# A two-block transformer kernel on one core: the first projection cut at 336, another order of the mixer's stages, one planner round

## The chip, the cores and the metric

One NeuronCore of a Trainium2 chip runs the whole program. The metric is the time of one execution on the device in microseconds (us). Each version is run several times and the median is taken; one more execution is taken with the hardware profiler, and all rows below come from it.

## The reference, cut to what matters

256 tokens of width 1024 go through a first block and then through a second block that is two layers deep. The change touches the first block's mixer and the end of the program:

```
h = rmsnorm(x, norm_mix_g)
c_q, c_kv, k_r, u_ssm, x_q, gate_logits = split(h @ w_in)    # 384, 256, 32, 512, 512, 3 x 1024 columns
y_a = mla_branch(c_q, c_kv, k_r, ...) @ w_o_mla              # 8 heads, causal
y_b = s5_branch(u_ssm, ...) @ w_o_ssm                        # state space scan, GELU, gated unit
y_c = cross_branch(x_q, mem, ...) @ w_o_cross                # 4 heads over 256 memory rows
gates = sigmoid(gate_logits + b_gate)
x = x + (gates[0] * y_a + gates[1] * y_b + gates[2] * y_c) @ w_out
x = x + convolved_swiglu(rmsnorm(x))
for l in range(2):
    x = x + 0.5 * swiglu(...); x = x + mixer2(...); x = x + 0.5 * swiglu(...)
return rmsnorm(x, g_final)
```

All is float32. The first 672 columns of `w_in` are c_q, c_kv and k_r.

## The kernel before, in words

The tokens are two tiles of 128 rows. Every product is made in three matmuls: a weight and an activation are each split into a high part (rounded to the matmul's format, a copy on ScalarE, ACT) and a low part (the rest, a subtraction on VectorE, DVE), and high x high, high x low and low x high are added up in PSUM. Weights come from memory in pieces of 512 KB (`weights`, five buffers `raw`, all issued by SyncE, SP) and are split into tiles `wh` and `wl`, of which 34 are in use at most; all working tiles share 65 slots.

The program isn't issued as it is written. The functions of `Ctx` only record operations (`Program.add`), with their engine, an assumed cost and what they depend on. At the end `issue` has a planner (`plan`) find an order: `backward` gives each operation a due time, `forward` places operations engine by engine in a simulated time, the most urgent first, as far as buffers allow. With two rounds this is done twice, the second time from the order of the first. The result is one fixed order for each engine's queue. So the string `ORDER`, which lists the stages of the first mixer in the order in which they are recorded, moves instructions on all engines.

The stages in `ORDER` (function `mixer1`, L1305): `h0` and `h1` are four heads each of the attention with latents (a product with `w_q_b` from the latent cq, a product with `w_kv_b` from ckv, head norms, rotary terms, scores `ms`, softmax `p`, output `mo`). `k0` and `k1` are the keys and values of the memory rows, `x0` the cross attention (`cs`, `co`). `s0` and `s1` are the halves of the state space branch: its maps `xB`, `x0`, `cT` are made on DVE and GpSimd (POOL) from small tables and transposed on TensorE (PE); u is moved by 16 small DMAs into `u4`; the products `se` give the state inputs, DVE turns them (`sp`), scans them (`sv`) and turns them back (`sg`), and PE multiplies `sg` with `cT` into `yb`. `g0`, `g1`, `g2` are the gates: 192 matmuls of 256 columns each (`proj_T`, tile `pt`), which depend on h and their weights alone. `b0`, `b2` are the first two branches into the merge.

Ahead of the stages `mixer1` loads x, warms PE up with matmuls of zeros (`warm_up`, L623), makes h (`first_norm`), and computes the first 672 columns with `proj`, the 512 columns of u with `proj_T`, the latents (`mla_latents`), the query of the cross attention and the norm of the memory rows (`norm_T`). The two calls for the 672 columns:

```python
        ps = self.proj(w_in, 0, 512, rows=True)
        ps = self.proj(w_in, 512, 160)
```

At the end of the program (L1590 on) `norm_rows` scales the rows of each token tile by their gain and norm in two halves `xs`, and SP stores them.

Of the kernel before, what the change touches and what calls it, by code (L numbers as in the profile page):

```python
# [13 lines left out]
AF = mybir.ActivationFunctionType  # L14
ALU = mybir.AluOpType
# [13 lines left out]
SLOW = 1.0  # L29
ORDER = "s0 h0 k0 k1 x0 h1 s1 g0 g1 g2 b0 b2"  # L30
STEPS = [1, 2, 3, 4] + [4 * q for q in range(1, 9)] + [32 * p for p in range(8)]
# [43 lines left out]
class Program:  # L75
# [281 lines left out]

    def issue(self, tc, rounds=2):
        with tc.manual_schedule():
            for i in self.plan(rounds):  # L360
                self.ops[i].call()
# [44 lines left out]
class Ctx:  # L406
# [40 lines left out]
    def load(self, dst, src, kind="load"):  # L447
        n = int(np.prod(src.shape))
        self.prog.add("sp", lambda: self.nc.sync.dma_start(dst, src), n * 4 / self.prog.DMA_RATE, [src], [dst], kind)


# [124 lines left out]

    def norm_rows(self, halves, g):

# [7 lines left out]
        r = self.row_rstd(ss)  # L586
        for b in range(2):
            self.dve.tensor_scalar(out=xs[b], in0=xs[b], scalar1=r, scalar2=None, op0=ALU.mult)
        return xs
# [33 lines left out]
    def warm_up(self, n):  # L623

        z = self.w("warm", 320).bitcast(BF16)
        self.dve.memset(z, 0.0)
        ps = self.bank("warm")
        for i in range(n):
            self.prog.add("pe", lambda: self.nc.tensor.matmul(ps, lhsT=z[:, 0:128], rhs=z[:, 128:640], start=True, stop=True),  # L629
                          430.0 if i < 9 else 220.0, [z], [ps], "first")  # L630

# [673 lines left out]
    def mixer1(self):  # L1305
# [7 lines left out]
        self.prog.ops[-1].kind = "first"  # L1313
        self.warm_up(19)
        self.parameters()
# [18 lines left out]
        self.pool.tensor_copy(out=self.identb, in_=self.ident)  # L1334
        ps = self.proj(w_in, 0, 512, rows=True)
        for t in range(2):
            self.act.copy(out=cq[t], in_=ps[t][:, 0:384])
            self.act.copy(out=ckv[t][:, 0:128], in_=ps[t][:, 384:512])
        ps = self.proj(w_in, 512, 160)
        for t in range(2):  # L1340
            self.act.copy(out=ckv[t][:, 128:288], in_=ps[t])

# [227 lines left out]
def two_block_kernel(ctx, tc, a, out):  # L1570
# [20 lines left out]
    for t in range(2):  # L1591
        xs = k.norm_rows(k.x_halves(t), g)
        for b in range(2):
            k.load(out[t * 128:t * 128 + 128, b * 512:b * 512 + 512], xs[b], "store")
    k.prog.issue(tc)
# [74 lines left out]
```

## Time and profile before

| what | us |
|---|---|
| median of 3 runs (lowest to highest) | 1574.74 (1571.79 to 1578.25) |
| the profiled execution | 1573.03 |
| its span in the profile | 1571.3 |
| PE busy in it | 1553.6 |
| DVE busy | 1025.7 |
| ACT busy | 840.1 |
| POOL busy | 101.7 |

The span is the profiled execution without what lies around it (1.7 us). Matmuls are pipelined: the next one starts before the last one has left the array, and their ends are modelled, so PE counts as busy where it is not at its peak. How many instructions start in a stretch says more. Of TensorE's clock the profile gives the granted share: 1.00 is 2.4 GHz, 0.50 is 1.2 GHz. A number in brackets behind a row of the timeline is the idle time of that engine ahead of it, with what ended it.

### The profile page before, as it was taken

The page shows a single profiled execution, that of the slowest core. Times are in us where ns is not written, and L with a number is a line of the kernel's source. Part 1 is how long each engine was busy: PE and PEld are TensorE (multiplying, and loading weights), DVE is VectorE, ACT ScalarE, POOL GpSimd, SP SyncE. Part 2 cuts the span into 40 slices and gives each one's busy share as a digit, 9 for nine tenths or more (in the row PEclk, how much of TensorE's full clock was granted, in tenths as well). Part 3 has the DMA queues.
Part 4 walks back from the last instruction along what each step waited for, and adds up shares of the span by engine and source line. Part 5 has one row for each costly group of instructions (what it writes and reads, how often), then busy time and mean ns, then how long its engine had stood idle before and what let it go on. Part 6 is the DMA issues. An engine that isn't in the chain of part 4 may idle for free.

```text
span 1571.3 us, 28497 instructions
## 1 busy us (share of the span) xinstructions
PE 1553.6 (99%) x11145; PEld 1430.9 (91%) x11145; DVE 1025.7 (65%) x1820; ACT 840.1 (53%) x1759; POOL 101.7 (6%) x204
## 2 busy tenths in 40 slices
PE   9999999999999999999999999999999999999998
PEld 7889999899989999889998999899998899989997
DVE  7896897787676545756657554665457656575543
ACT  8766665765555544555446444455345554464442
POOL 5114600000000000000000000000000000000000
PEclk9999999999999999999999999999999999999999
DMA  8556164566556656555647665466664556476650
GB/s 284 174 151 178 44 211 138 191 217 212 185 175 221 208 195 210 158 158 164 212 138 235 200 208 193 148 221 203 207 209 148 167 162 198 146 233 209 203 186 28
DMA packets 214230, 287.79 MB, mean 183 GB/s; under 512 B 13904, under 2 KB 170192, under 8 KB 214096
## 3 DMA queue, kind: packets, MB, share of 16 engines
q1 hardware_dynamic: 213952, 285.71, 57.0%
q8 instruction: 88, 1.44, 0.4%
q14 instruction: 46, 0.38, 0.1%
q10 hardware_dynamic: 144, 0.26, 0.0%
HBM read 284.36 MB, written 1.05 MB: 182 GB/s over the span
## 4 chain that ended last, share of the span: by engine, by line
PE 89%; DVE 4%; ACT 2%; DMA 2%; issue 1%; POOL 0%; POOLq 0%; DVEq 0%; ACTq 0%
PE pt L497 50%; PE acc L497 21%; PE pr L497 7%; PE up L497 4%; PE tr L522 2%; ACT wh L398 1%; DVE wl L398 1%; DMA raw<-in_w_ffn_dram 1%; DVE xs L398 1%; DMA raw<-in_w_in_dram 1%; DVE x L398 1%; PE se L497 1%; PE ms L497 0%; PE warm L629 0%; PE yb L497 0%
## 5 line engine op out<-in xcount | busy, mean ns | idle before, releaser
L398 DVE TENSOR_TENSOR wl<-raw,wh 128x512 fp32r<-128x512 f32 x1045 | 657.2, 686 | 193.9 <-ACT wh L398 184.0
L497 PE MATMUL pt<-h,wh 128*128 128x256 f32 x4224 | 736.1, 277 | 0.0
L398 ACT CAST wh<-raw 128x512 fp32r<-128x512 f32 x1045 | 578.3, 618 | 147.2 <-DMA raw<-in_w_in_dram 43.3
L497 PEld LDWEIGHTS pt<-h,wh 128*128 128x128 f32 x4224 | 642.4, 188 | 2.8 <-issue 0.2
L497 PE MATMUL pt<-h,wl 128*128 128x256 f32 x2112 | 584.1, 277 | 0.0
L497 PEld LDWEIGHTS pt<-h,wl 128*128 128x128 f32 x2112 | 397.0, 188 | 0.7 <-issue 0.5
L497 PE MATMUL acc<-wh,gh 128*128 128x512 f32 x440 | 170.6, 388 | 0.0
L497 PE MATMUL acc<-wh,gl 128*128 128x512 f32 x440 | 170.6, 388 | 0.0
L497 PE MATMUL acc<-wl,gh 128*128 128x512 f32 x440 | 170.4, 387 | 0.0
L497 PE MATMUL pr<-wh,h 128*128 128x512 f32 (+2 forms) x480 | 130.8, 355 | 2.4 <-DVE h L398 2.3
L398 ACT CAST gh<-sg 128x512 fp32r<-128x512 f32 x47 | 29.2, 621 | 147.5 <-DVE sg L398 147.5
L497 PE MATMUL up<-wh,h 128*128 128x512 f32 x320 | 100.8, 390 | 0.1
L497 PEld LDWEIGHTS pr<-wh,h 128*128 128x128 f32 x480 | 84.5, 188 | 16.0 <-DVE h L398 2.5
L497 PEld LDWEIGHTS acc<-wh,gl 128*128 128x128 f32 x440 | 82.6, 188 | 17.0
L497 PEld LDWEIGHTS acc<-wl,gh 128*128 128x128 f32 x440 | 82.5, 188 | 16.0
L497 PEld LDWEIGHTS acc<-wh,gh 128*128 128x128 f32 x440 | 82.6, 188 | 15.9
L398 DVE TENSOR_TENSOR sg<-sg,pt 128x512 f32<-128x512 f32 x36 | 24.8, 688 | 110.1 <-PE pt L497 110.1
L398 ACT ACTIVATE sg<-pt 128x512 f32<-128x512 f32 x36 | 21.5, 598 | 130.4 <-PE pt L497 130.4
L497 PE MATMUL pr<-wl,h 128*128 128x512 f32 (+2 forms) x240 | 85.0, 354 | 0.0
L398 POOL TENSOR_TENSOR rs<-s,mhalf 128x1 f32<-128x1 f32 x20 | 16.4, 820 | 961.8 <-DVE s L398 961.8
L497 PEld LDWEIGHTS up<-wh,h 128*128 128x128 f32 x320 | 59.7, 188 | 12.5 <-ACT h L398 0.6
L398 ACT ACTIVATE junk<-x 128x512 f32<-128x512 f32 x36 | 22.7, 631 | 79.1 <-DVE x L398 76.2
(352 smaller groups left out, 1639.8 us busy)
## 6 DMA issues: line engine op xcount, KB each, us to landing
raw<-in_w_ffn_dram SPq DMA_DIRECT2D x264, 512.0 KB, 5.0
raw<-in_w_in_dram SPq DMA_DIRECT2D x124, 512.0 KB, 5.0
raw<-in_w_up_dram SPq DMA_DIRECT2D x44, 512.0 KB, 4.8
raw<-in_w_out_dram SPq DMA_DIRECT2D x24, 512.0 KB, 4.8
raw<-in_w_down_dram SPq DMA_DIRECT2D x22, 512.0 KB, 4.5
raw<-in_w_mem_kv_dram SPq DMA_DIRECT2D x8, 512.0 KB, 4.5
raw<-in_w_branch_ret_dram SPq DMA_DIRECT2D x8, 512.0 KB, 3.5
raw<-in_w_o_mla_dram SPq DMA_DIRECT2D x4, 512.0 KB, 3.5
```

The lines of the kernel that those rows point to most:

```text
L398: self.prog.add(self.name, lambda: getattr(self.eng, op)(**kw), self.cost(op, kw), list(aps.values()), writes, "fast" if self.name == "dve ...
L497: self.prog.add("pe", lambda: self.nc.tensor.matmul(ps, lhsT=lhsT, rhs=rhs, start=start, stop=stop), ns, [lhsT, rhs], [ps])
L522: self.prog.add("pe", lambda: self.nc.tensor.transpose(out, src, ident), 109, [src, ident], [out])
```

## The change

Four things. The first 672 columns of `w_in` are computed as two parts of 336 columns, not as 512 and 160; the high parts are copied out of PSUM accordingly. The warm-up has 17 products of zeros, not 19. At the end, the second half of the second token tile is scaled on ACT, not on DVE, and stored from ACT's queue. `ORDER` is another one, with g0 and g1 earlier and k0, k1, x0 later, and the planner makes one round in place of two.

```diff
-ORDER = "s0 h0 k0 k1 x0 h1 s1 g0 g1 g2 b0 b2"
+ORDER = "s0 g0 h0 h1 g1 s1 k0 k1 x0 g2 b0 b2"
...
-    def issue(self, tc, rounds=2):
+    def issue(self, tc, rounds=1):
...
+    def store(self, dst, src, own):
+        eng, queue = ("aq", self.nc.scalar) if own else ("sp", self.nc.sync)
+        self.prog.add(eng, lambda: queue.dma_start(dst, src), 65536 * 4 / self.prog.DMA_RATE, [src], [dst], "store")
...
-    def norm_rows(self, halves, g):
+    def norm_rows(self, halves, g, shared=False):
...
-            self.dve.tensor_scalar(out=xs[b], in0=xs[b], scalar1=r, scalar2=None, op0=ALU.mult)
+            if shared and b == 1:
+                self.act.activation(out=xs[b], in_=xs[b], func=AF.Copy, scale=r)
+            else:
+                self.dve.tensor_scalar(out=xs[b], in0=xs[b], scalar1=r, scalar2=None, op0=ALU.mult)
...
-                          430.0 if i < 9 else 220.0, [z], [ps], "first")
+                          427.0 if i < 13 else 214.0, [z], [ps], "first")
...
-        self.warm_up(19)
+        self.warm_up(17)
...
-        ps = self.proj(w_in, 0, 512, rows=True)
+        ps = self.proj(w_in, 0, 336, rows=True)
         for t in range(2):
-            self.act.copy(out=cq[t], in_=ps[t][:, 0:384])
-            self.act.copy(out=ckv[t][:, 0:128], in_=ps[t][:, 384:512])
-        ps = self.proj(w_in, 512, 160)
+            self.act.copy(out=cq[t][:, 0:336], in_=ps[t])
+        ps = self.proj(w_in, 336, 336)
         for t in range(2):
-            self.act.copy(out=ckv[t][:, 128:288], in_=ps[t])
+            self.act.copy(out=cq[t][:, 336:384], in_=ps[t][:, 0:48])
+            self.act.copy(out=ckv[t], in_=ps[t][:, 48:336])
...
-        xs = k.norm_rows(k.x_halves(t), g)
+        xs = k.norm_rows(k.x_halves(t), g, t == 1)
         for b in range(2):
-            k.load(out[t * 128:t * 128 + 128, b * 512:b * 512 + 512], xs[b], "store")
+            k.store(out[t * 128:t * 128 + 128, b * 512:b * 512 + 512], xs[b], t == 1 and b == 1)
```

What this does to the order, at three places on DVE. First the scan of s0. Before, as DVE's queue has it from the last weight splits ahead of the scan on:

```order
L398 TENSOR_TENSOR wl<-raw,wh 128x512 x2
L398 TENSOR_TENSOR sp<-se,turn 128x512 x4
L398 TENSOR_TENSOR sp<-sp 128x512 x2
L398 SCALAR_TENSOR_TENSOR sv<-decay,sp 128x512 x2
L398 TENSOR_TENSOR sg<-sv,turn 128x512 x4
L398 TENSOR_TENSOR sg<-sg 128x512 x2
L398 TENSOR_TENSOR wl<-raw,wh 128x512 x9
```

Now (`rr` belongs to the rotary tables, `kss` to the latents, `rs_m` and `q` to the heads' norms):

```order
L398 TENSOR_SCALAR rs_m<-hs 128x4
L398 TENSOR_TENSOR sp<-se,turn 128x512 x2
L398 TENSOR_REDUCE kss<-krq 128x1 x2
L398 SCALAR_TENSOR_TENSOR rr<-rk,rr 128x32
L398 TENSOR_TENSOR sp<-se,turn 128x512 x2
L398 TENSOR_TENSOR sp<-sp 128x512 x2
L398 SCALAR_TENSOR_TENSOR sv<-decay,sp 128x512 x2
L398 TENSOR_TENSOR sg<-sv,turn 128x512 x4
L398 TENSOR_TENSOR sg<-sg 128x512 x2
```

The two splits right ahead of the scan are gone, and the splits for the gates that followed it follow later. On PE, 39 gate products stand between the last `se` and the first `yb<-sg` before, and 22 now, four of them of g1.

Second, the splits of the weights of h0 (`wl` of 384 columns is from `w_q_b`, the `wl` of 512 columns that follow are from `w_kv_b`). Before:

```order
L398 TENSOR_TENSOR wl<-raw,wh 128x384 x3
L398 TENSOR_TENSOR pw<-pw,pv 128x320
L398 TENSOR_TENSOR wl<-raw,wh 128x512
L398 TENSOR_SCALAR pk<-pw 128x320
L398 TENSOR_TENSOR wl<-raw,wh 128x512
L398 TENSOR_TENSOR pv<-pw,pk 128x320
L398 TENSOR_TENSOR wl<-raw,wh 128x512
L398 TENSOR_SCALAR pk<-pw 128x320
L398 TENSOR_TENSOR wl<-raw,wh 128x512
```

Now (`h` is the low part of the memory's rows, `pm` and `cT` are the maps of s0):

```order
L398 TENSOR_TENSOR wl<-raw,wh 128x384 x3
L398 TENSOR_TENSOR h<-tr,h 128x4x128 x4
L398 TENSOR_TENSOR pm<-sbc,pwr 128x512 x3
L398 TENSOR_TENSOR cT<-pm 64x16x16 x3
L398 TENSOR_TENSOR pm<-sbc,pwr 128x512
L398 TENSOR_TENSOR cT<-pm 64x16x16 x5
L398 TENSOR_TENSOR wl<-raw,wh 128x512 x2
```

The splits of the two weights of h0 stood four operations of the state branch's tables apart; now the memory's rows and the maps for C stand between them. On PE the two products follow each other with two gate products between them.

Third, the maps `xB` of s1, beside the softmax of h0. Before:

```order
L398 RECIPROCAL ls<-ls 128x4
L398 TENSOR_TENSOR p<-p,ls 128x512
L398 TENSOR_TENSOR xB<-pm 64x16x16 x2
L398 TENSOR_TENSOR q<-q,rs_r 128x384
L398 TENSOR_SCALAR rs_m<-hs 128x4
L398 TENSOR_TENSOR wl<-raw,wh 128x512
L398 TENSOR_TENSOR xB<-pm 64x16x16 x6
```

Now:

```order
L398 TENSOR_TENSOR xB<-pm 64x16x16
L398 TENSOR_TENSOR p<-p,ls 128x512
L398 TENSOR_TENSOR xB<-pm 64x16x16
L398 RECIPROCAL ls<-ls 128x2
L398 TENSOR_TENSOR p<-p,ls 128x512
L398 TENSOR_TENSOR xB<-pm 64x16x16 x4
L398 TENSOR_TENSOR kk<-kv,rs_r 128x4x64
L398 TENSOR_TENSOR xB<-pm 64x16x16 x2
```

The weight split `wl` between the maps is gone, and the maps have moved into the softmax of h0's second token tile. On SP the 32 moves of u, which stood in six blocks between loads of weights, stand in two blocks of 16. From the first norm behind the mixer on, PE's order is as before but for the five places where a norm begins.

## Rows read from the trace of the kernel before

**Rows 1.** The page, part 1: engine, busy us (share of the span), instructions.

```profile
PE 1553.6 (99%) x11145; PEld 1430.9 (91%) x11145; DVE 1025.7 (65%) x1820; ACT 840.1 (53%) x1759; POOL 101.7 (6%) x204
```

**Rows 2.** Busy time by windows: us, PE, PEld, DVE, ACT, POOL (instructions), granted clock, DMA.

```profile
60.00:70.00 10.00, 10.00 (x47) 8.26 (x46) 9.96 (x20) 6.32 (x27) 0.00 (x0) 1.00 0.28 83
...
130.00:140.00 10.00, 10.00 (x90) 10.00 (x89) 6.51 (x12) 7.34 (x12) 4.76 (x8) 1.00 0.64 173
140.00:150.00 10.00, 9.59 (x84) 9.34 (x83) 6.30 (x13) 6.91 (x20) 5.98 (x15) 1.00 0.44 116
150.00:160.00 10.00, 8.14 (x66) 7.45 (x66) 5.31 (x13) 5.70 (x13) 4.98 (x15) 1.00 0.28 92
160.00:170.00 10.00, 8.90 (x68) 7.87 (x66) 8.30 (x21) 4.96 (x10) 5.90 (x11) 0.67 0.18 55
```

**Rows 3.** Waits of PE: who waited for whom, us, times, longest.

```profile
PE pr L497 <- DVE h L398: 2.3, 1, 2.3
PE tr L522 <- DVE ckv L398: 1.4, 1, 1.4
```

**Rows 4.** The chain in order of time: start, us, what.

```profile
60.14 10.45 PE pr L497 x46
...
110.94 27.91 PE pt L497 x242
```

**Rows 5.** Timeline of the start: start, us, engine, line, operation, out<-in.

```profile
1.25 6.83 PE L629 MATMUL warm<-warm 128*128 128x512 bf16 x19 [1.25 <-DVE warm L392]
...
6.79 1.62 DVE L398 TENSOR_SCALAR xs<-x,rs 128x512 f32<-128x512 f32 x2 [0.73 <-POOL rs L398]
...
8.72 0.88 ACT L398 ACTIVATE h<-tr,par 128x128 fp32r<-128x128 f32 x3
...
22.63 0.27 PE L497 MATMUL pr<-wl,h 128*128 128x160 f32 x1
22.65 0.46 ACT L398 CAST wh<-raw 128x320 fp32r<-128x320 f32 x1
...
27.87 0.44 PE L497 MATMUL pt<-h,wh 128*128 128x256 f32 x2
```

**Rows 6.** Timeline around the scan of s0.

```profile
99.61 1.08 PE L497 MATMUL kT<-cT,x 128*32 128x128 f32 x32
99.61 2.48 DVE L398 TENSOR_TENSOR sp<-se,turn 128x512 f32<-128x512 f32 x4
...
101.65 2.51 PE L497 MATMUL yb<-uT,kT 128*128 128x256 f32 x16
...
108.68 2.26 PE L497 MATMUL yb<-sg,cT 128*32 128x63 f32 x128 [0.86 <-DVE sg L398]
```

**Rows 7.** Timeline of the late stage: h0's softmax and the maps of s1.

```profile
146.45 0.22 PE L497 MATMUL ms<-cmask,identb 128*128 128x128 bf16 x1
...
150.93 0.63 PE L522 MATMUL tr<-par,p 128*128 128x128 f32 x4 [1.34 <-DVE p L398]
...
156.33 0.69 DVE L398 TENSOR_TENSOR wl<-raw,wh 128x512 fp32r<-128x512 f32 x1 [3.71 <-PE pt L497]
...
157.05 0.52 POOL L392 MEMSET xB<- 128x512 f32 x1 [4.46 <-PE pt L497]
```

**Rows 8.** The end: two rows of the timeline, then the stores (duration ns min/median/max).

```profile
1565.38 0.63 ACT L398 ACTIVATE junk<-x 128x512 f32<-128x512 f32 x1 [1.84 <-DVE x L398]
...
1567.02 0.88 DVE L398 TENSOR_SCALAR xs<-xs,rs 128x512 f32<-128x512 f32 x2 [0.66 <-POOL rs L398]
...
L449 SPq DMA_DIRECT2D out_dram<-xs x4: 332/343/378, 1562.2 to 1568.0; - x4
```

**Rows 9.** Timeline where the first merge ends and the next norm begins.

```profile
277.40 0.58 ACT L398 CAST h<-tr 128x512 fp32r<-128x512 f32 x1
...
277.57 0.60 PE L522 MATMUL tr<-par,xs 128*128 128x128 f32 x4
278.03 0.49 PE L497 MATMUL up<-wh,h 128*128 128x512 f32 x1
```

## Prediction

> **What bounds the kernel now.** I read the page first: TensorE (PE) is busy for 1553.6 of 1571.3 us [rows 1], so a gain has to shorten what PE executes or close a hole in it. Then the busy time by windows, since busy time hides holes between pipelined matmuls; there the number of PE instructions says more. In 130 to 140, where PE runs gate products back to back, a window of 10 us holds 90 instructions; in 140 to 170 the three windows hold 84, 66 and 68 [rows 2]. That is 52 missing of 270, at 0.11 us each 5.8 us, and in the last of the three the granted clock is 0.67: half the clock (1.2 in place of 2.4 GHz) for about two thirds of the window, some 3.4 us of these 5.8. After 270 the windows are full; so the room lies in the first mixer, up to 215, and at the program's end. VectorE (DVE) is what PE runs after in the first 110 us: it is busy for 9.96 us of 60 to 70 [rows 2]. The waits of PE name the single places: 2.3 us for the norm of the memory rows, 1.4 us for a latent [rows 3], 1.3 us for softmax weights [rows 7].
>
> **The change, part by part.**
>
> *First 672 columns.* Before, 48 matmuls of 512 columns and 48 of 160. The chain shows 46 matmuls of 512 columns in 10.45 us, 0.227 each, and 242 of 256 in 27.91, 0.115 each [rows 4]; the 48 of 160 columns take from 22.63 to 27.87, 0.109 each [rows 5], no less than those of 256. So 48 x 0.227 + 5.24 = 16.1 us. Afterwards 96 of 336 columns; the line through 256 and 512 columns gives 0.150 each, 14.4 us. That is -1.7 us of PE work. ScalarE (ACT) and DVE split the same columns in 16 pieces in place of 11, a 320-column cast costing 0.46 us [rows 5]; the chain runs partly through them before 22 us, so I take -1.6, with 0 (they set the pace) and -2.5 (an early wait of PE goes too) as ends. The Trainium skill (TensorE: Matmul & The Clock Gate, Back-to-back issue gap) has a rule that speaks against this edit: a matmul costs its columns at 2.4 GHz plus 2.5 ns. By it 160 columns are 69 ns and both forms cost the same 13.7 us; the 0.109 measured [rows 5] decides against it.
>
> *Two products of zeros less.* They end at 8.08, the scaled rows that PE needs next are half done at 7.6, and the first split of them starts at 8.72 on ACT [rows 5]. Nothing, at best -0.4.
>
> *Last scaling on ACT, last store from ACT's queue.* The two scalings end at 1567.90, one after the other; an ACT pass over 512 columns takes 0.63 us [rows 8], so it ends at 1567.65 and its store leaves 0.25 us sooner, and without waiting for the third store's issue. -0.3, between -0.5 and 0.
>
> *One round of the planner.* From 270 on PE's order is the same but for five places where a residual is followed by a norm. Where a merge ends (three of them) the transposes of the first token tile now stand behind the last product instead of around it. The copy of h takes 0.58 us and the next product starts right behind it [rows 9]; it used to lie under the other four transposes and three products, now only under four transposes (0.44). About 0.25 us of new wait at each, some of it back because the last product ends earlier: +0.5 in all, 0 to +1.
>
> *The mixer's new order, up to the first state product.* Ahead of the products of the states s0 with C (108.68 [rows 6]) PE now has no k0 and k1 (96 x 0.227 = 21.8 us), four products of h1 less (0.9), 1.7 less from the first part, and 124 more gate products (14.3): 10.1 us less. DVE has 16 splits of k0 and k1, one of h1 and seven map operations less, at 0.62 each [rows 6] 14.9, and nine gate splits more, 5.6: 9.3 us less. DVE leads here, so PE arrives earlier and waits about 0.8 us more than now. By places: the 2.3 and 1.4 us [rows 3] go, since gate products, not k0, now follow the memory's norm, and the latents' transposes stand behind 96 products. In their place PE waits for the splits of h0's second weight, which stand on DVE behind the split of the memory's rows and the maps for C (16 operations, some 8 us by their widths). PE, which I estimate 2 us behind DVE there, has 11 products in that time (1.7 us): about 4 us. And between the last state input and the state products PE has 17 gate products fewer (2.0 us): now the scan's chain takes 99.61 to 108.68 [rows 6], against 5.9 us of cover. +1.0. PE's own work up to 108.68 adds up to 92.5 us at these durations and starts at 8.1, so its waits up to there are now 8.1 us. The ends: -3, if only the start (2 us) and this chain (3.2 us) still hold PE up, and +3, if DVE also waits for h0's loads, which now stand on SP behind two blocks of 16 moves of u, at 0.34 us of issue and more each [rows 8] 5.5 us a block.
>
> *The mixer's late stage.* This is the largest term. Before, PE stood 1.34 us for the softmax weights: 4.3 us from the last score to the transpose [rows 7], covered by 25 instructions. Now 39 gate products and 15 others (6 us) lie there; so too for the copy behind it. Then a weight split on DVE waited 3.71 us and a fill of xB on GpSimd (POOL) 4.46 us, each for PE to release a buffer [rows 7], PE came to the transposes of xB too early, and the clock fell behind them [rows 2]. In the new order no split stands on DVE between the first and the last xB, and these lie between the softmax steps of h0. I take back the clock's 3.4 us and half of the other 2.4, 4.6 together, rounded down: -4.5. The ends: 0 (waits of the same size turn up for x0, which is now last) and -7.5 (nothing is lost from 140 to 210).
>
> Sum: -1.6 + 0 - 0.3 + 0.5 + 1.0 - 4.5 = -4.9 us. The profiled execution took 1573.0 us (span 1571.3); the median of the runs shown is 1.7 higher, 1574.7, so I forecast 1569.8, -0.3%. About 0.5% (7.9 us, 1566.9 to 1582.6) is what a measurement of this kernel tells from no change.
>
> **The rivals.**
>
> *The first mixer closes up.* Every term at its good end: -2.5 - 0.4 - 0.5 + 0 - 3 - 7.5 = -13.9, 1560.8 us. For it: PE has work without dependences (g0, g1, g2) between all stages. Against it: the 60 to 70 row, where DVE has nothing left to give [rows 2], and the thinner cover of the scan.
>
> *The waits only move.* The late stage loses the same: -0.4, so 1574.3. For it: the instructions of h0, h1, x0 and s1 are the same, and the lengths of their chains too; x0 has only the branch b0 beside it. Against it: the cover counted above.
>
> *PE idles early, and the clock falls there.* Slower: around h0's second weight and in front of the state products, DVE's queue holds PE for some 4 and 3 us with nothing else issued. It decides if the clock falls in one of these holes as it did behind 150 to 160, where 66 instructions ran [rows 2]. Price: -1.6 - 0.3 + 0.5 + 3 for the waits, +3.4 for one more fall of the clock at the price of 160 to 170, and nothing gained later: +5.0, 1579.7. The Trainium skill (TensorE: Matmul & The Clock Gate, What's actually happening) has the half clock as the default that only activity lifts. The trace agrees: the granted clock falls once in mid-program, behind its two thinnest windows. Against this rival: the 2.3 us hole ahead of 58.8 [rows 3] brought no fall.
>
> **How the numbers follow.** Forecast 0.48, closing up 0.20, waits that move 0.17, early holes with the clock 0.15. All cases but closing up stay mostly within 0.5%: faster by over 0.5% comes from closing up (0.19) and from the forecast's good end (0.12), 0.31; slower by over 0.5% from the early holes' bad end and a little beyond, 0.07; the same 0.62. The range goes from 1560, the closing up, to 1581, the early holes with a margin of 1 us for the worst start; the forecast's own is 1564 to 1574.
>
> **What would show it.** Right: 160 to 170 at a full clock; about 85 or more PE instructions in each 10 us window of the late stage; no wait of PE for the memory's h; a wait of some 3 us in front of the products of the states. The first 672 columns end 1.5 us earlier. Wrong: a clock under 1 in a window before 110; PE waiting for POOL's or DVE's xB as before; a hole at x0; a changed time behind 290, where I expect no more than 1 us.

## The result, and the profile after

The changed kernel takes 1582.97 us (median of 6 runs, 1581.12 to 1587.91), the kernel before 1574.43 beside it. The ratio on record, 1.0064 with an interval of 1.0047 to 1.0081, is not the quotient of these two medians (that is 1.0054, within the interval); the table below gives it for every run. So the changed kernel is **slower by 0.6%**, where I had forecast 0.3% faster and a range up to 1581. The profiled execution took 1582.9 us, its span is 1581.1.

PE has no more to do than before [rows 1]; the page of the changed kernel, part 1:

```profile
PE 1555.1 (98%) x11143; PEld 1434.9 (91%) x11143; DVE 1024.9 (65%) x1824; ACT 842.9 (53%) x1765; POOL 99.9 (6%) x204
```

So the time went into holes. Its windows, with the columns of [rows 2]:

```profile
10.00:20.00 10.00, 8.26 (x38) 7.99 (x39) 9.34 (x30) 8.99 (x30) 3.02 (x10) 0.66 0.79 245
...
60.00:70.00 10.00, 10.00 (x85) 9.75 (x84) 2.29 (x6) 4.61 (x14) 0.00 (x0) 1.00 0.34 74
70.00:80.00 10.00, 2.40 (x8) 1.69 (x9) 9.54 (x20) 8.79 (x25) 1.72 (x4) 0.67 0.52 177
80.00:90.00 10.00, 10.00 (x59) 9.47 (x58) 6.61 (x13) 7.35 (x38) 2.07 (x6) 0.82 0.65 199
...
110.00:120.00 10.00, 9.25 (x173) 8.80 (x174) 9.28 (x21) 4.30 (x21) 6.87 (x2) 0.83 0.57 164
...
160.00:170.00 10.00, 10.00 (x91) 9.95 (x89) 3.76 (x8) 7.31 (x18) 4.53 (x12) 1.00 0.46 131
170.00:180.00 10.00, 10.00 (x90) 9.34 (x88) 6.96 (x18) 7.76 (x19) 4.05 (x8) 1.00 0.02 5
```

The late stage became what I had forecast: 91 and 90 instructions a window from 160 to 180 at the full clock, where 68 [rows 2] and 88 ran before:

```profile
170.00:180.00 10.00, 10.00 (x88) 9.90 (x88) 7.51 (x17) 6.31 (x15) 7.32 (x10) 0.98 0.01 2
```

But in the changed kernel, from 70 to 80 PE issues 8 instructions, and the granted clock is 0.67 there and 0.82 in the next window. In the window ahead of it DVE, which I had called the engine that leads, is busy for 2.29 of 10 us. The waits of PE (who for whom: us, times, longest) name the place:

```profile
PE pr L501 <- DVE wl L398: 7.6, 2, 6.3
PE up L501 <- ACT h L398: 3.2, 5, 1.3
PE yb L501 <- DVE sg L398: 2.1, 1, 2.1
```

The first is h0's second weight, the second the norms behind the merges, the third the states of s0; the waits of before that stood here are gone [rows 3]. The timeline around the first, queue by queue:

```profile
39.31 10.35 SPq L449 DMA_DIRECT2D u<-uT  x16
...
52.70 13.32 SPq L449 DMA_DIRECT2D u<-uT  x16
66.11 0.53 SPq L449 DMA_DIRECT2D raw<-in_w_q_b_dram  x1
66.75 0.38 SPq L449 DMA_DIRECT2D raw<-in_w_kv_b_dram  x1
...
68.73 0.51 ACT L398 CAST wh<-raw 128x384 fp32r<-128x384 f32 x1 [5.39 <-DMA raw<-in_w_q_b_dram]
...
69.28 0.56 DVE L398 TENSOR_TENSOR wl<-raw,wh 128x384 fp32r<-128x384 f32 x1 [7.71 <-ACT wh L398]
69.76 2.48 DVE L398 TENSOR_TENSOR h<-tr,h 128x512 fp32r<-128x512 f32 x4
...
75.86 2.18 DVE L398 TENSOR_TENSOR cT<-pm 64x256 f32<-64x256 f32 x5
78.07 1.45 DVE L398 TENSOR_TENSOR wl<-raw,wh 128x512 fp32r<-128x512 f32 x2
...
71.98 0.50 PE L501 MATMUL pr<-wh,ckvh 128*128 128x512 f32 x1 [1.25 <-ACT wh L398]
78.82 0.79 PE L501 MATMUL pr<-wl,ckvh 128*128 128x512 f32 x1 [6.35 <-DVE wl L398]
...
110.75 3.68 PE L501 MATMUL yb<-sg,cT 128*32 128x63 f32 x128 [2.10 <-DVE sg L398]
```

SP issues the 16 moves of s1's u in 13.32 us. Two of h0's three loads, those in the rows above, stand behind them; ACT waits for the first of these, and DVE, idle for 7.71 us, waits for ACT. Then DVE does the memory's rows and the maps (16 operations, 69.76 to 78), and only then splits the weight for which PE waits since 72.5. Together PE waits 7.6 us at this weight (1.25 and 6.35). Two marks sum the profile up. The products of the states start at 110.75 (108.68 before [rows 6]), although by the prediction's count PE has 8.4 us less to do ahead of them (k0 and k1 less, gates more) besides the first columns. And the first norm behind the mixer begins here, 7.5 us later than before (276.4):

```profile
283.89 1.03 PE L526 MATMUL tr<-par,xs 128*128 128x128 f32 x8
285.77 0.49 PE L501 MATMUL up<-wh,h 128*128 128x512 f32 x1 [0.84 <-ACT h L398]
```

Behind that mark come 2.4 us more: 1290.2 us to the last product, where it was 1287.8.

The start lost time as well. The first gate product, behind the 672 columns, starts at 30.04, not at 27.87 [rows 5]:

```profile
10.45 0.42 PE L501 MATMUL pr<-wh,h 128*128 128x336 f32 x1 [1.98 <-ACT h L398]
...
13.33 0.65 PE L501 MATMUL pr<-wl,h 128*128 128x336 f32 x1 [1.29 <-DVE wl L398]
...
30.04 0.39 PE L501 MATMUL pt<-h,wh 128*128 128x256 f32 x2
```

### The profile page after: what moved, and what is told of

Same layout as the page of the kernel before. It is cut to its first block, busy times and chain, and to the rows that moved or that the text cites. A ratio compares the mean times of both kernels' runs of the same rounds, so it can differ in the third digit from the quotient of the medians.

```text
span 1581.1 us, 28523 instructions
## 1 busy us (share of the span) xinstructions
PE 1555.1 (98%) x11143; PEld 1434.9 (91%) x11143; DVE 1024.9 (65%) x1824; ACT 842.9 (53%) x1765; POOL 99.9 (6%) x204
## 4 chain that ended last, share of the span: by engine, by line
PE 89%; DVE 3%; DMA 2%; ACT 1%; issue 1%; POOL 0%; POOLq 0%; ACTq 0%; SPq 0%; DVEq 0%
PE pt L501 48%; PE acc L501 20%; PE pr L501 7%; PE up L501 7%; PE tr L526 2%; DVE wl L398 1%; DMA raw<-in_w_ffn_dram 1%; DMA raw<-in_w_in_dram 1%; PE yb L501 1%; DVE x L398 1%; PE ms L501 0%; PE glu L501 0%; PE ry L501 0%; ACT wh L398 0%; DVE xs L398 0%
## 5 line engine op out<-in xcount | busy, mean ns | idle before, releaser
L398 DVE TENSOR_TENSOR wl<-raw,wh 128x512 fp32r<-128x512 f32 (+2 forms) x1050 | 656.2, 682 | 207.0 <-ACT wh L398 191.0
L398 ACT CAST wh<-raw 128x512 fp32r<-128x512 f32 (+2 forms) x1050 | 578.3, 616 | 144.4 <-DMA raw<-in_w_ffn_dram 51.9
```

Source lines behind the costliest of these rows:

```text
L398: self.prog.add(self.name, lambda: getattr(self.eng, op)(**kw), self.cost(op, kw), list(aps.values()), writes, "fast" if self.name == "dve ...
```

## The experiments

Of every run the table gives the ratio to the kernel before, timed beside it on the same chip, and two marks of its profile: where the first norm behind the mixer begins, and from there to the last product. The marks are of one execution each, and executions of one kernel differ in their granted clock (last section), so a few us between two marks can be that; the ratios come from all runs.

| kernel | ratio (interval) | median us | mixer ends | behind |
|---|---|---|---|---|
| before | 1 | 1574.4 | 276.4 | 1287.8 |
| the change | 1.0064 (1.0047 to 1.0081) | 1583.0 | 283.9 | 1290.2 |
| late_moves | 1.0063 (1.0040 to 1.0086) | 1583.2 | 282.3 | 1290.6 |
| dve_first | 1.0081 (1.0063 to 1.0099) | 1586.0 | 287.3 | 1290.6 |
| moves_dve | 1.0061 (1.0046 to 1.0076) | 1584.5 | 282.2 | 1291.9 |
| idle_moves | 1.0029 (1.0018 to 1.0040) | 1577.1 | 276.8 | 1292.0 |
| idle_moves_dve | 1.0020 (1.0009 to 1.0031) | 1575.8 | 276.9 | 1289.8 |
| three_fixes | 1.0282 (1.0265 to 1.0299) | 1619.9 | 273.3 | 1337.6 |
| no_hole_clock | 1.0038 (1.0025 to 1.0051) | 1581.2 | 279.3 | 1290.8 |
| zeros_19 | 1.0062 (1.0040 to 1.0083) | 1583.0 | 280.8 | 1290.8 |
| two_rounds | 1.0049 (1.0032 to 1.0065) | 1581.5 | 288.2 | 1288.6 |
| old_order | 1.0092 (1.0075 to 1.0108) | 1589.8 | 289.8 | 1292.2 |
| after_512 | 1.0053 (1.0035 to 1.0071) | 1580.9 | 281.5 | 1290.6 |
| after_null | 1.0073 (1.0054 to 1.0092) | 1584.0 | 285.2 | 1289.8 |
| before_336_tail | 1.0074 (1.0050 to 1.0098) | 1585.0 | 288.1 | 1288.5 |
| cut_336_old_queues | 1.0035 (1.0024 to 1.0047) | 1580.1 | 285.5 | 1288.8 |
| before_new_order | 1.0061 (1.0044 to 1.0078) | 1582.7 | 285.2 | 1288.3 |
| before_one_round | 1.0139 (1.0119 to 1.0158) | 1594.6 | 294.4 | 1290.0 |
| before_null | 1.0036 (1.0017 to 1.0055) | 1579.5 | 281.4 | 1289.5 |
| before_move_cost | 1.0029 (1.0019 to 1.0038) | 1577.7 | 280.2 | 1289.2 |

**The hole, from three sides.** late_moves takes the finished order and puts the 16 moves of s1's u behind seven loads of weights:

```diff
+        late = [i for i, op in enumerate(self.ops) if op.kind == "move"][16:]
+        sp = [i for i in order if self.ops[i].eng == "sp"]
+        anchor = sp[sp.index(max(late, key=sp.index)) + 7]
+        order = [i for i in order if i not in late]
+        p = order.index(anchor) + 1
+        order[p:p] = late
```

> The changed kernel (1583.0 us) with one block of 16 moves of u, those of s1, on SyncE's queue behind the first weights of h0 and h1 in place of ahead of them; every other engine's order is the same. In the changed kernel PE stands 8.0 us at h0's second weight (70.4 to 78.8 us), and the granted clock is at half for the 10.2 us after. Theory A (the weights stand behind the moves on SyncE): that hole falls below 3 us, the clock doesn't fall at 73 us, 1574 to 1577. Rival B (the hole is VectorE's order, the splits stand behind the memory's rows and the maps for C, earlier weights don't help): hole over 6 us, 1580 to 1583. Rival C (what is gained there is waited for at the scan of s0, since VectorE leads): hole below 3 us but the wait ahead of the products of the states grows from 2.1 us by as much, 1580 to 1584.

dve_first moves the 16 DVE operations behind the splits of h0's second weight (`kv`, two operations):

```diff
+        p = min(dve.index(i) for i in kv)
+        late = dve[p - 16:p]
+        order = [i for i in order if i not in late]
+        p = max(order.index(i) for i in kv) + 1
+        order[p:p] = late
```

> The changed kernel (1583.0 us) with the two splits of h0's second weight on VectorE ahead of the memory's rows and the maps for C (16 operations, 8.3 us) in place of behind them; all queues otherwise the same, the weights arrive as late as before. Theory A (late weights and VectorE's order make the hole together): PE waits only until the weight is there and split, 72.5 us, a hole of some 2.5 us in place of 8.0, no fall of the clock at 73, 1575 to 1578. Rival B (the late weights alone): the hole stays over 5 us, 1581 to 1583. Rival C (VectorE idles 2 us more, so the scan of s0 comes later): hole 2.5 us, but the products of the states wait 2 to 6 us longer, 1580 to 1584.

moves_dve has both edits.

> The changed kernel (1583.0 us) with both moves at once: the s1 moves of u behind h0's and h1's first weights on SyncE, and the splits of h0's second weight ahead of the memory's rows and the maps on VectorE. One alone left a hole of 4.0 us and the other of 8 us, and neither changed the time. Theory A (the hole at h0's second weight costs the time, if it is closed for good): no wait over 1.5 us there, no half clock between 60 and 90, 1574 to 1577. Theory C (a chain from the projections of h0 over VectorE's maps and ScalarE's copies sets when the products of the states can start, about 110 us, whatever PE waits for first): the hole is gone, waits of the same size appear ahead of the state inputs or the state products, 1580 to 1584.

None was faster. In late_moves PE's wait at h0's second weight fell from 7.6 to 4.0 us, in moves_dve to 2.5, and the time stayed. In dve_first it is no shorter than in the change (8.2), with another cause: PE's product waits for ACT's gates, which stand behind seven casts of later weights. I take it that the gates release the bank of PSUM that the product needs, since the memory's rows, now behind the splits on DVE, keep others; that is an inference, not a row.

```profile
72.89 0.80 PE L508 MATMUL pr<-wl,ckvh 128*128 128x512 f32 x1 [4.01 <-DVE wl L405]
...
PE pr L509 <- ACT gate L406: 8.2, 1, 8.2
...
72.90 0.50 PE L515 MATMUL pr<-wh,ckvh 128*128 128x512 f32 x1 [2.48 <-ACT gate L412]
```

(The rows are of late_moves, of dve_first's waits, and of moves_dve.)

I took the unchanged time of moves_dve for the chain of DVE (theory C), but the timeline of moves_dve shows something else:

```profile
75.12 10.88 SPq L463 DMA_DIRECT2D u<-uT  x16
86.10 30.32 SPq L463 DMA_DIRECT2D raw<-in_w_in_dram  x8
...
90.44 0.62 ACT L412 CAST wh<-raw 128x512 fp32r<-128x512 f32 x1 [7.90 <-DMA raw<-in_w_in_dram]
...
95.89 0.92 PE L515 MATMUL se<-u,bT 128*128 128x64 f32 x4 [3.72 <-ACT bT L412]
```

The moves now stand ahead of the next piece of gate weights. ACT waits 7.90 us for it, the copies of the maps `bT` are queued behind that cast, and PE waits 3.72 us for them. The block made the next one late. In the changed kernel SP issues no load from 87 to 113 us; idle_moves puts the moves there (11 in place of 7 in the edit above), idle_moves_dve with the order on DVE as well.

> The changed kernel (1583.0 us) with the 16 moves of u of s1 four loads further back on SyncE than in late_moves: behind the last weights of h1 and four pieces for the gates, where SyncE issues no load for some 25 us. In moves_dve the piece for the gates behind the moves came at 86.1 us, ScalarE waited 7.9 us for it with the copies of the maps bT queued behind, and PE 3.7 us for these copies. Theory A2 (the block of moves, 10 to 13 us of SyncE, makes late whatever stands behind it; in its idle time it costs nothing): the hole at h0's second weight is 4 us as in late_moves, no wait of PE for bT over 1 us, and the first mixer ends 4 to 6 us earlier than in the changed kernel: 1577 to 1579. Rival C (VectorE's own chain sets the products of the states at 110 us): 1581 to 1584.

> The same with the splits of h0's second weight ahead of the memory's rows and the maps on VectorE as well. Theory A2: neither the hole at h0's second weight (under 3 us, the banks that the memory's rows hold) nor the wait for bT; the products of the states start at 103 to 106 us in place of 110.7, and the time is 1574 to 1577. Rival C: PE waits for the maps in front of the state inputs or products instead, these start at 109 us or later, 1580 to 1584.

Now the time falls, from 1.0064 to 1.0029 and 1.0020, and these intervals lie below that of the change. The mixer ends at 276.8 and 276.9, 7 us earlier, and in idle_moves_dve the states' products start at 104.07:

```profile
82.09 12.07 SPq L463 DMA_DIRECT2D u<-uT  x16
...
104.07 2.26 PE L515 MATMUL yb<-sg,cT 128*32 128x63 f32 x128 [2.15 <-DVE sg L412]
```

Of the 7 us some 3 are the start: in these two profiles the clock didn't fall there, and the first gate product starts at 27.26 and 27.03 in place of 30.04, with the same instructions ahead of it. From that product to the mixer's end it takes 253.9 us in the change, 249.6 and 249.9 here, so some 4 us go with the place of the moves. By the ratios the place of this one block on SP is worth about half of the loss (0.35 of 0.64%); theory C falls. What the other half is made of stays open in part: 0.20% (0.09 to 0.31) remain in idle_moves_dve, of which the 2.0 us more behind the mixer (1289.8 for 1287.8) would be 0.13. The wait in front of the states remains too (2.15 us). In idle_moves_dve PE still waited 3.5 us for ACT's gates at h0's second weight, as in dve_first; so three_fixes puts the splits behind the memory's rows but ahead of the maps (`dve[p - 12:p]`), and takes the order of all that is recorded behind the mixer from two rounds of the planner (each engine's own order, filled into the places that one round had given that engine).

```diff
+        late = dve[p - 12:p]
...
+            slots = [q for q, i in enumerate(order) if self.ops[i].eng == e and i >= self.behind]
+            key.update(zip((i for i in orders[2] if self.ops[i].eng == e and i >= self.behind), slots))
```

> The changed kernel with the moves of u of s1 in SyncE's idle time (as in idle_moves), the splits of h0's second weight on VectorE behind the memory's rows but ahead of the 12 operations of the maps for C (in idle_moves_dve they stood ahead of the memory's rows too, and PE waited 3.5 us for a bank that these held), and behind the mixer the order of two rounds of the planner in place of one. Theory A2 and the 2.3 us of the single round behind the mixer: no wait over 1.5 us at h0's second weight and no half clock there, the first mixer ends at 271 to 274 us (276.9 in idle_moves_dve, 283.9 in the changed kernel, 276.4 before), 2 us less behind it: 1568 to 1572, faster than both kernels. Rival (VectorE's chain to the products of the states takes the gain): the first mixer ends at 276 to 277, 1573 to 1574.

Its first mixer is the best of all: no wait at h0's second weight, full clock there, and the first norm begins at 273.35, 10.5 us earlier than in the change and 3.1 earlier than before, in its windows and timeline:

```profile
70.00:80.00 10.00, 10.00 (x72) 9.69 (x71) 9.84 (x23) 9.96 (x44) 3.68 (x7) 1.00 0.47 147
```

```profile
273.35 1.03 PE L556 MATMUL tr<-par,xs 128*128 128x128 f32 x8
```

Behind the mixer my merge of two orders failed: 47 us more, lost in both mixers of the second block. The waits of PE:

```profile
PE tr L556 <- DVE xs L428: 18.4, 10, 5.1
PE tr L556 <- DVE rr L428: 12.1, 4, 3.1
```

With 1290.2 us behind the mark and 7.0 from the last product to the end, as in the change, this first mixer would give a span of some 1570.5. That is an estimate; the kernel without the merge was not timed, and no version that beats the kernel before was measured.

**The clock.** no_hole_clock repeats the first product of h0's second weight (`again`) 27 times in the hole.

```diff
+                if i == first:
+                    for _ in range(27):
+                        again()
                 self.ops[i].call()
```

> The changed kernel (1583.0 us) with the first product of h0's second weight issued 27 times more (27 x 0.227 = 6.1 us) in the hole of 6.6 us behind it, so that PE isn't idle there; nothing else is moved, the result is overwritten by the same product. Theory A (the hole costs its length and a fall of the clock behind it): no half clock from 73 to 84, the products from 78.8 on take their full pitch, and the time falls by the 2.3 us that the slower pitch took from 78.8 to 83.6: 1580 to 1581. Rival B (VectorE and ScalarE pace what follows, the clock of PE is worth nothing there): 1582.5 to 1584.

```profile
70.00:80.00 10.00, 9.14 (x41) 7.37 (x42) 8.43 (x19) 8.15 (x21) 2.15 (x5) 1.00 0.39 136
80.00:90.00 10.00, 10.00 (x71) 9.64 (x70) 7.59 (x16) 8.03 (x46) 4.56 (x9) 1.00 0.81 256
```

The repeated products fill the hole, the clock stays full, and 71 instructions run from 80 to 90 where there were 59. The ratio falls from 1.0064 to 1.0038, though these intervals overlap. In this profile the clock didn't fall at 12 and 111 us either, and the first gate product starts at 27.04, 3.0 us earlier than in the change; so most of its 4.6 us at the end of the mixer are not the filled hole's. From the first gate product to the states' products it takes 80.1 us, 80.7 in the change: the filled hole and the full clock behind it are worth some 0.6 us there, where I had expected 2.3. The median, 1581.2, lies between the ranges of A and B, and what the fall of the clock behind the hole costs stays open.

zeros_19 issues two more products of zeros behind the 17:

```diff
+        last = lambda: (zero(), zero(), zero())
...
+            self.prog.add("pe", last if i == n - 1 else zero,
```

> The changed kernel (1583.0 us) with two more products of zeros behind the 17, the order otherwise the same. In the changed kernel the granted clock is at half from 11.9 to 18.7 us, which the kernel before doesn't show. Theory A (the shorter warm-up lets the clock fall): no half clock before 20 us, the first 672 columns end 2 to 3 us earlier, 1580 to 1581. Rival B (PE's hole of 2.0 us ahead of the first product, which waits for ScalarE's h, and the wait of 1.3 us behind it make the clock fall): the hole begins 0.4 us later, the clock falls as before, 1583.

The time is the same, 1583.0. The clock fell at the start again (12.9 to 16.3), whereas in late_moves, with 17 zeros and the same start, it didn't. Nothing shows that the shorter warm-up costs time; whether the clock falls at the start differed between executions with the same instructions there.

**The parts and the planner.** Three runs each set one input of the changed kernel back, or change the kernel before in part, and let the planner order everything anew.

```diff
-    def issue(self, tc, rounds=1):
+    def issue(self, tc, rounds=2):
```

> The changed kernel (1583.0 us) with two rounds of the planner in place of one, the new order of the mixer's stages kept. Theory A (one round sets the moves of u in two unbroken blocks ahead of h0's weights, and lets the norms behind a merge wait): the moves stand between weight loads again, no hole over 3 us at h0's second weight, and the program behind the mixer takes 2 us less: 1572 to 1576. Rival B (the order of the stages costs it, whatever the rounds): 1579 to 1582, only the 2 us behind the mixer go.

```diff
-ORDER = "s0 g0 h0 h1 g1 s1 k0 k1 x0 g2 b0 b2"
+ORDER = "s0 h0 k0 k1 x0 h1 s1 g0 g1 g2 b0 b2"
```

> The changed kernel (1583.0 us) with the old order of the mixer's stages, all else as changed (336 columns, 17 zeros, tail on two engines, one round). Theory D (the new order of the stages is what costs): 1572 to 1576, the first mixer ends within 1 us of the kernel before (276.4 us at the first norm behind it). Rival E (the single round, with its unbroken blocks of moves of u, or the start costs): 1579 to 1584.

before_336_tail is the kernel before with the two parts of 336 and the tail, and nothing else of the diff.

> The kernel before (1574.4 us) with the two parts of 336 columns and the last scaling and store on ScalarE and its queue alone (19 zeros, old order of stages, two rounds). Theory (by the prediction's terms): -1.6 and -0.3, 1572.5. Rival (ScalarE and VectorE pace the first 672 columns, which ended at 28.1 us in the changed kernel without a fall of the clock, 27.9 in the kernel before): 1574 to 1575. Third: the planner makes another order of everything behind, by up to 5 us either way.

two_rounds came out where its rival B had it (1581.5, within 1579 to 1582), and its interval overlaps that of the change; the other two missed every range. The old order of stages with the rest of the change is the slower one (1.0092), and the cut with the tail costs 0.74% in the kernel before. Yet the first 672 columns do end 1.5 us earlier there, as forecast: the gates start at 26.34, not at 27.87 [rows 5].

```profile
26.19 0.31 PE L501 MATMUL pr<-wh,h 128*128 128x336 f32 x1
26.34 0.39 PE L501 MATMUL pt<-h,wh 128*128 128x256 f32 x2
```

That left two theories: F, the planner's new order costs, whatever input brought it about; G, the cut itself. Four more, by the lines of the diff shown already: the new `ORDER` alone in the kernel before; the two calls with 512 and 160 columns back in the changed one; a null; `rounds=1` alone in the kernel before.

> The kernel before (1574.4 us) with the new order of the mixer's stages alone (512 and 160 columns, 19 zeros, two rounds). With the parts of 336 columns the old order gave 1585.0 (two rounds) and 1589.8 (one), the new one 1581.5 and 1583.0: there the new order of stages gains 3.5 to 7 us. Theory G (the new order of stages is good, the cut at 336 is what costs, some 10 us through the order that the planner makes with it): 1567 to 1573. Theory F (any new input makes the planner write another order of the first mixer, and that of the kernel before is a lucky one): 1579 to 1586.

> The changed kernel (1583.0 us) with 512 and 160 columns again, all else as changed (new order of stages, one round, 17 zeros, tail on two engines). Theory G (the cut at 336 costs): 1572 to 1576. Theory F (the planner's order is as good or bad as chance has it): 1579 to 1587.

> The kernel before (1574.4 us) with nothing changed but the planner's own assumed costs of the 19 products of zeros (427 ns for the first 13 and 214 for the others in place of 430 for the first 9 and 220), so every instruction is the same and only the order of some 650 of PE's first 1535 operations is another. Theory F (the planner's order of the first mixer is a matter of chance by several us): 1578 to 1585. Theory G (the parts themselves make the difference): 1573 to 1576.

> The kernel before (1574.4 us) with one round of the planner alone. Behind the mixer I read 2.3 us more in the changed kernel (some 0.4 to 1.7 us at the transposes of the norms behind the merges): so at least 1576.5 by either theory. Theory F: 1580 to 1590. Theory G: 1576 to 1578.

before_null has the instructions of the kernel before; only the planner's assumed costs of the zeros differ:

```diff
-                          430.0 if i < 9 else 220.0, [z], [ps], "first")
+                          427.0 if i < 13 else 214.0, [z], [ps], "first")
```

It is slower by 0.36% (0.17 to 0.55). So another order alone, with not one instruction changed, can cost about half of what the change lost; how much of the change's own loss is of this kind, that doesn't show. before_new_order, after_512 and before_null all came out in theory F's ranges and outside G's; before_one_round, a single round with the old stages, loses most (1.0139) and lies above both ranges. after_null does the same to the changed kernel, before_move_cost lets the planner count 750 ns for the issue of a move, not 450:

```diff
-                        free[e] = t + self.DMA_ISSUE
+                        free[e] = t + (750.0 if op.kind == "move" else self.DMA_ISSUE)
```

> The changed kernel (1583.0 us) with the planner's assumed costs of the 17 products of zeros as before (430 and 220 in place of 427 and 214), every instruction the same. In the kernel before a change of these numbers alone cost 5 to 7 us. Theory F: the order is again another, and the time lies anywhere from 1578 to 1588; with the new order of stages, which puts products without dependences between the stages, the spread is smaller (its four versions so far lie within 1580.9 to 1583.0): 1580 to 1585. Theory G (the planner's orders of the changed kernel are all alike, only the kernel before is sensitive): 1582 to 1584.

> The kernel before (1574.4 us) with one number of the planner changed: 750 ns for the issue of a move of u in its forward pass, not 450 (the trace has 0.65 to 0.83 us for each), so that it doesn't put 16 moves ahead of a load as if they were nearly free. Theory H (the planner's wrong cost of the moves makes the bad orders): 1570 to 1574. Theory F (any other order than the lucky one of the kernel before is worse, whatever the reason for it): 1578 to 1586.

With the new stages all four combinations of rounds and cut, and the null, lie between 1.0049 and 1.0073; with the old ones between 1 and 1.0139. Among these the new order of stages spreads less, and the kernel before is the best of the six with the old stages; whether that is luck or its settings were chosen by time is not on record. after_null, at 1584.0, lies in F's range and on the edge of G's, and decides nothing. A better price of the moves gives the best of the replanned old orders (1.0029), but not one as good as before's: at 1577.7 it lies between the ranges of H and F.

cut_336_old_queues makes the cut alone and keeps every queue as it was, by a table.

```diff
+            for d in json.loads(zlib.decompress(base64.b64decode(TABLE))):
+                i += d
+                self.ops[i].call()
```

> The kernel before with the two parts of 336 columns alone, and every other instruction on every engine in the order of the kernel before (written out as a table, so that the planner has no say; only the latents' norms, which now need the second part, come a little later). With the planner's own order the same cut took 1585.0 us, 10.6 more than before (1574.4). Theory F (the parts cost nothing by themselves, the order that the planner makes of them does): 1571.5 to 1575, the first 672 columns end 1.5 us earlier (26.3 in place of 27.9), no hole over 3 us behind. Theory G (the cut itself delays the latents, and with them h0): 1578 to 1586.

Its 1580.1 us (1.0035) lie in the range of theory G: with every queue as it was, the cut does cost something of its own. The first 672 columns end at 29.73, not at the 26.3 that I had expected, and the timeline (of the slowest of its 11 runs) shows waits for ACT in them and for the latents behind them:

```profile
24.69 0.42 PE L501 MATMUL pr<-wh,h 128*128 128x336 f32 x1 [1.56 <-ACT wh L402]
...
31.73 0.55 PE L526 MATMUL tr<-par,cq 128*128 128x128 f32 x3 [1.38 <-DVE cq L402]
...
35.19 0.90 PE L526 MATMUL tr<-par,cq 128*128 128x128 f32 x3 [2.45 <-DVE cq L402]
```

The 384 columns of cq lay in the first part of 512; cut at 336 they end in the second, and their norm starts later. PE waits 3.8 us for them, where it had waited 1.4 for ckv [rows 3]. In the changed kernel gate products stand there, and the wait doesn't show; with 512 and 160 columns (after_512) it is at 1.0053, not clearly apart from 1.0064. So both theories hold in part: the order alone can cost 0.36%, and the cut, in the old order, 0.35%.

## Why the prediction was wrong

**The step that failed** is the mixer up to the first state product, +1.0 between -3 and +3. By the prediction's terms the states' products would have started at 108.68 - 8.4 - 1.6 + 1.0 = 99.7 us; they start at 110.75, 11.1 later. Of these, 3.8 are already there at the first gate product (30.04, where -1.6 would give 26.3), which is the term of the first columns, below. The other 7.3 are this step's: from the first gate product to the states' products it takes 80.7 us, 80.8 before, with 8.4 us less work, so +8.3 in place of +1.0. The place was right (h0's second weight on DVE behind the memory's rows and the maps, "about 4 us"; 7.6 measured, with the clock at half from 73 to 84 us behind it) and so was the reason that would make it worse, the loads behind "two blocks of 16 moves of u", which I kept as the bad end. Its price was wrong: I took 0.34 us of issue from the last stores [rows 8], 5.5 us a block, where the blocks take 10.35 and 13.32, on average up to 0.83 a move. The trace of before had the price, in SyncE's timeline:

```profile
37.93 4.48 SPq L449 DMA_DIRECT2D u<-uT  x5
...
43.64 1.88 SPq L449 DMA_DIRECT2D u<-uT  x3
```

I didn't look for the row of the same transfer. With 13 us in place of 5.5 the late loads were no longer the bad end but the likely case. idle_moves bears it out: the same kernel with the second block elsewhere gives back about half of the loss. The sum itself was loose, too: the places that I listed add up to -2.3 - 1.4 + 4 + 2.3 (3.2 in place of 0.86 at the scan) = +2.6, not +1.0; at the scan PE waited 2.10.

**The rival that came true** is the early hole with the fall of the clock, at 1579.7 and a chance of 0.15. Its place and its mechanism are what the profile shows; the hole was 7.6 us where it has 4, and the clock fell in three stretches of the profile (10 to 20, 70 to 90, 110 to 120), not one. That it came near the time is in part luck: it had nothing gained later, and the late stage did gain 3.0. The case was likelier than I gave it. The one hole that I had set against it was 2.3 us long. And the fall of the clock in the kernel before did not come behind its thinnest windows, as I wrote: PE is busy for 7.74 us of 50 to 60, with 55 instructions, less than in 150 to 160 [rows 2], and the clock stays full there and in the next window [rows 2]:

```profile
50.00:60.00 10.00, 7.74 (x55) 7.12 (x54) 7.72 (x13) 8.71 (x32) 6.35 (x12) 1.00 0.82 246
```

**The other terms.**
- First 672 columns, -1.6: +2.2 in the changed kernel's profile (30.04 for 27.87). The products cost what the line between 256 and 512 columns says, and they end 1.5 us earlier in before_336_tail. The formula of the Trainium skill (TensorE: Matmul & The Clock Gate, Back-to-back issue gap), by which both forms cost the same, isn't borne out at 160 columns (0.109 measured, 0.069 by it); the section itself calls it the gap of an isolated matmul and too low for few columns. In the changed kernel PE's first product waits 1.98 us for ACT, a later one 1.29 for DVE, and the clock is at half from 11.9 to 18.7; late_moves, with the waits and without the fall, is at 28.13. So ACT and DVE pace the start, the end of the range that I had put at 0, and the clock comes on top. What I overlooked is that the cut runs through cq.
- Two zeros less, 0: no effect shows (zeros_19).
- Tail, -0.3: nothing. From the start of the last scalings to the end it takes 4.28 us before [rows 8] and 4.26 now. The store does leave earlier, 0.75 us after the start of the scalings where the last one left 0.98 after it before. But from issue to landing this store takes 2.5 us, where those of before took 2.0 to 2.3:

```profile
1576.84 0.72 ACT L398 ACTIVATE xs<-xs,rs 128x512 f32<-128x512 f32 x1 [0.90 <-POOL rs L398]
...
1577.59 0.35 ACTq L453 DMA_DIRECT2D out_dram<-xs  x1
```

- One round, +0.5: 2.4 behind the mixer. The kernels with one round need 1289.8 to 1292.2 us from the mark to the last product, those with two 1287.8 to 1289.5 (three_fixes, with its own merge, apart). The new wait is the one I named, `up` for the copy of h, but it is 3.2 us over five places and up to 1.3 each, not 0.25. Inside the first mixer I had given the round no price of its own, and there it was worth far more (before_one_round, +18 us at the mark).
- The late stage, -4.5: from the states' products to the norm it takes 173.1 us, 167.8 before, with 8.4 us more work: -3.0. The mechanism was right; 1.4 us of the difference is the states' products themselves, which ran at half the clock (3.68 us, 2.26 before); without that the term would have been -4.4.

Early +10.5 (2.1 later with 8.4 less to do), late -3.0, behind +2.4, tail 0: 9.9, against 9.8 between the spans (the difference is rounding).

## What to carry to other kernels

Price the issue of a DMA by the row of the same kind of DMA, and count a block of small ones as what it is for an in-order queue: 13 us in which no weight is loaded. Moving such a block makes late what then stands behind it; it cost least where its queue was otherwise idle. And where a planner orders the program, first time a change of its assumed costs alone: if that moves the time by several us, no part of a change can be priced without the order that comes with it.

## What the runs showed of the hardware that was not expected

The moves of u, 16 KB each, took SP 0.65 to 0.83 us on average over the two blocks of the change (0.59 to 0.97 for a single issue), against 0.37 for most pieces of 512 KB. And the clock fell at the start in some executions and not in others with the same instructions there (the change at 11.9 us, late_moves not at all before 72). So one kernel has a spread of its own, and it goes with the clock: of the 11 runs of cut_336_old_queues the fastest, 1575.1, has a mean granted clock of 0.998, the slowest, 1583.1, one of 0.994, and the others lie between.
